# One Strassen level in the second feed-forward of a two-block transformer kernel

## The chip, the cores and the metric

One core of a Trainium2 chip runs the whole kernel in one launch. The metric is the device time of one execution in microseconds (us). Times are medians of several executions; the profile is one execution of its own, so its span differs a little from the median.

## What is computed

Two transformer blocks on 1024 tokens of width 1024, all in float32. The first has two attentions and a gated feed-forward, the second two mixers (a gated spatial one and a gated linear attention) and the feed-forward that is changed here:

```python
    h = h + rmsnorm(m, post_mix_g[l])
    f = rmsnorm(h, pre_ff_g[l]) @ w_ff1[l]
    f = jnp.square(jax.nn.relu(f)) @ w_ff2[l]
    h = h + rmsnorm(f, post_ff_g[l])
```

`w_ff1` is 1024 x 4096 and `w_ff2` is 4096 x 1024. Every product is kept close to float32 by splitting each operand into a rounded part (hi) and the rest (lo), both of type float32r, and adding three products: hi x hi, hi x lo and lo x hi.

## The kernel before

`mm3` (L153 to L156) issues the three matmuls of one 128x128 block of weights against 512 moving columns, so all matmuls of the feed-forward have lines 154, 155 and 156. A split is a copy (hi) and a subtraction (lo): for weights that is `split_rows` (L158 to L167), for transposed tokens `to_T` (L186 to L196), for the hidden values L1413 and L1414.

The second output product (L1350 to L1392) goes over eight token tiles t. For each it does 16 `out2` groups of three matmuls into a 1024-wide PSUM tile (two buffers), then on the vector and scalar engines a root mean square over the tile (L1386, `rstd_ssq`), scaling (L1388), the residual (L1389), a store of the new residual to DRAM (L1390) and the norm of the next stage (`Norm`, L836 and L838). While tile t+1 is multiplied, at group `X_FIN` = 15, `pend.finish()` transposes tile t with eight transposes on the tensor engine and splits it into `hcur`, the token operand of the feed-forward. The token operand thus grows along with the product, and tile 7 is finished after the first hidden blocks have begun (L1416 to L1420).

The second feed-forward (L1403 to L1499) takes the 32 blocks of 128 hidden columns in pairs, the last four together. For a pair, `ff1` (L1406) makes hidden x token tiles: per half of the tokens and per block, 8 `mm3` into one PSUM bank, then relu and square on the scalar engine (L1411, L1412), hi on the vector engine and lo on GpSimd. `ff2` (L1437) multiplies them with two rows of blocks of `w_ff2`: for each token tile t 4 `mm3`, and L1463 adds the PSUM tile to `fr[t]`, which stays in SBUF. Hidden values never leave the chip. The weights of the next pair are loaded (512 KB each, queue SP) and split while the current pair is multiplied. The last four blocks (L1465 on) end each token tile with the last norm (L1490 to L1498) and the store (L1499).

Matmuls of the feed-forward: 32 x 2 x 8 x 3 = 1536 for the first product and 32 x 8 x 2 x 3 = 1536 for the second, 3072 in all.

The program text is an order of issue, but the order in which each engine's stream was laid out is a scheduler's: it places instructions by when it expects their inputs and buffers, and the finished streams are fixed. A pool of tiles that is opened with `reuse_waits="tile"` waits for the former users of its bytes tile by tile; one without waits for all of the former pool.

## Time and profile before

| what | us |
|---|---|
| median of 3 runs | 2654.95 (2654.71 to 2658.44) |
| span of the profiled execution | 2657.4 |
| tensor engine busy in it | 2590.0 |
| start of the last matmul of the second output product | 1926.89 |
| start of the last matmul of the program | 2648.60 |

In the rows below PE is the tensor engine's matmuls, PEld its weight loads, DVE the vector engine, ACT the scalar engine, POOL GpSimd and SP the engine whose queue issues most DMAs. Matmuls overlap, so their pace is read from the distance of their starts and not from their durations.

### The profile page before, as it was taken

To read this page: it belongs to the slowest core of one execution; us is meant where nothing else is said; L and a number is where in the kernel's file an instruction comes from. 1 tells how busy PE (TensorE), PEld (TensorE's weight loads), DVE (VectorE), ACT (ScalarE), POOL (GpSimd) and SP (SyncE) were. 2 spreads that over 40 slices of the span, in tenths; PEclk is the share of its full clock that TensorE was granted. 3 is DMA by queue.
4 is the path that set the end of the run, shared out by engine and by line. 5 is a ranking of instruction groups with operands and counts; after the bars stand their busy time and mean duration, and the time that the engine had idled before them with its cause. 6 is when DMAs were issued, how large, how long until landed. Compare 5 with 4: busy or idle time off the path is not lost.

```text
span 2657.4 us, 34289 instructions
## 1 busy us (share of the span) xinstructions
PE 2590.0 (97%) x13228; PEld 2141.1 (81%) x13228; DVE 1310.0 (49%) x2790; ACT 958.4 (36%) x2241; POOL 589.8 (22%) x447
## 2 busy tenths in 40 slices
PE   7999999988899999999999999999999999999998
PEld 4889999977778888888888788777877878787886
DVE  7977878889763222222222423538544343333325
ACT  4776767778332111111111432345331111111122
POOL 2300000033124333333332210102022121212214
PEclk9999999999999999999999999999999999999999
DMA  7101212231523111111110230212231111111102
GB/s 264 45 28 54 61 52 64 64 99 52 185 75 92 48 48 48 48 48 48 48 48 9 94 87 1 68 40 72 88 127 48 48 48 48 48 48 48 48 32 103
DMA packets 147423, 174.20 MB, mean 66 GB/s; under 512 B 13342, under 2 KB 113582, under 8 KB 146236
## 3 DMA queue, kind: packets, MB, share of 16 engines
q1 hardware_dynamic: 144092, 160.48, 19.3%
q0 software_dynamic: 3168, 11.54, 1.3%
q8 instruction: 104, 1.70, 0.3%
q14 instruction: 59, 0.48, 0.1%
HBM read 155.19 MB, written 16.79 MB: 65 GB/s over the span
## 4 chain that ended last, share of the span: by engine, by line
PE 83%; DVE 8%; ACT 5%; issue 2%; DMA 1%; POOL 1%; SPq 0%; DVEq 0%; ACTq 0%; POOLq 0%
PE acc L154 15%; PE acc L156 14%; PE acc L155 14%; PE wide L154 9%; PE wide L156 9%; PE wide L155 9%; PE acc L601 2%; PE tr L577 2%; PE wide L543 2%; ACT qT L151 1%; PE tr L191 1%; ACT prob L564 1%; PE wide L283 1%; PE acc L615 1%; DVE fr L1498 1%
## 5 line engine op out<-in xcount | busy, mean ns | idle before, releaser
L156 PE MATMUL acc<-hT,slab 128*128 128x512 f32 x1216 | 480.2, 395 | 0.2 <-DVE slab L167 0.2
L154 PE MATMUL acc<-hT,slab 128*128 128x512 f32 x1216 | 479.2, 394 | 0.3 <-ACT hT L195 0.3
L155 PE MATMUL acc<-hT,slab 128*128 128x512 f32 x1216 | 479.4, 394 | 0.0
L154 PE MATMUL wide<-slab 128*128 128x512 f32 x1088 | 431.3, 397 | 1.0 <-DVE fr L1461 0.5
L156 PE MATMUL wide<-slab 128*128 128x512 f32 x1088 | 430.6, 396 | 1.1 <-POOL slab L911 1.1
L155 PE MATMUL wide<-slab 128*128 128x512 f32 x1088 | 428.2, 394 | 0.0
L164 ACT CAST slab<-st 128x1024 fp32r<-128x1024 f32 (+1 forms) x148 | 152.4, 1046 | 562.6 <-PE wide L156 449.6
L167 POOL TENSOR_TENSOR slab<-st,slab 128x1024 fp32r<-128x1024 f32 (+1 forms) x104 | 250.4, 2413 | 438.3 <-ACT slab L164 421.8
L155 PEld LDWEIGHTS acc<-hT,slab 128*128 128x128 f32 x1216 | 228.3, 188 | 54.8 <-DVE hT L196 0.4
L156 PEld LDWEIGHTS acc<-hT,slab 128*128 128x128 f32 x1216 | 228.3, 188 | 54.2 <-DVE slab L167 0.6
L154 PEld LDWEIGHTS acc<-hT,slab 128*128 128x128 f32 x1216 | 228.2, 188 | 54.2 <-ACT hT L195 0.6
L154 PEld LDWEIGHTS wide<-slab 128*128 128x128 f32 x1088 | 204.5, 188 | 54.5 <-DVE fr L1463 5.4
L156 PEld LDWEIGHTS wide<-slab 128*128 128x128 f32 x1088 | 204.7, 188 | 47.8 <-POOL slab L911 1.9
L155 PEld LDWEIGHTS wide<-slab 128*128 128x128 f32 x1088 | 204.6, 188 | 46.2
L1413 DVE CAST slab<-h 128x512 fp32r<-128x512 f32 x60 | 69.9, 1165 | 249.8 <-ACT h L1412 249.8
L1463 DVE TENSOR_TENSOR fr<-wide,fr 128x1024 f32<-128x1024 f32 x104 | 127.1, 1223 | 126.7 <-PE wide L156 125.8
L908 DVE TENSOR_TENSOR h<-h,acc 128x512 f32<-128x512 f32 x44 | 30.2, 687 | 305.0 <-PE acc L156 305.0
L983 DVE TENSOR_TENSOR xr<-wide,xr 128x1024 f32<-128x1024 f32 x88 | 107.7, 1224 | 134.9 <-PE wide L156 134.7
L154 PE MATMUL acc<-wi,slab 128*128 128x384 f32 (+1 forms) x480 | 167.9, 350 | 2.6 <-DVE y L142 1.3
L1414 POOL TENSOR_TENSOR slab<-h,slab 128x512 fp32r<-128x512 f32 x60 | 78.3, 1306 | 406.9 <-DVE slab L1413 406.9
L155 PE MATMUL acc<-wi,slab 128*128 128x384 f32 (+1 forms) x480 | 160.9, 336 | 0.5 <-DVE wi L235 0.5
L156 PE MATMUL acc<-wi,slab 128*128 128x384 f32 (+1 forms) x480 | 160.2, 335 | 0.2 <-POOL slab L327 0.2
(415 smaller groups left out, 4336.6 us busy)
## 6 DMA issues: line engine op xcount, KB each, us to landing
st<-in_w_ff_dram SPq DMA_DIRECT2D x62, 512.0 KB
wm<-in_w_mod_dram SPq DMA_DIRECT2D x48, 256.0 KB
st<-in_w_gate_dram SPq DMA_DIRECT2D x22, 512.0 KB
st<-in_w_up_dram SPq DMA_DIRECT2D x22, 512.0 KB
st<-in_w_down_dram SPq DMA_DIRECT2D x22, 512.0 KB
...
st<-in_w_in_dram SPq DMA_DIRECT2D x12, 512.0 KB
```

Source lines behind the costliest of these rows:

```text
L154: pe.matmul(ps, lhsT=l_hi, rhs=r_hi, start=first, stop=False)
L155: pe.matmul(ps, lhsT=l_hi, rhs=r_lo, start=False, stop=False)
L156: pe.matmul(ps, lhsT=l_lo, rhs=r_hi, start=False, stop=last)
L164: act.copy(w[:, 0], st)
L167: (pool if lo_eng == "pool" else dve).tensor_tensor(w[:, 1], st, fview(w[:, 0]), ALU.subtract)
L543: pe.matmul(Sps[:, o : o + ln], lhsT=qT[:, w_, :], rhs=R.kT[self.kh][:, src : src + ln], start=(w_ == 0), stop=(w_ == 1))
L577: pe.transpose(t[:, (j - b0) * P : (j - b0 + 1) * P], self.P_t[:, j * P : (j + 1) * P], ident)
L601: pe.matmul(OT, lhsT=R.V[self.kh][:, vt, :], rhs=self.PT[j // 4][:, j % 4].rearrange("p e t -> p (e t)"), start=(j == 0), stop=(j == nk_al ...
L983: dve.tensor_tensor(xr[t], ps, xr[t], ALU.add)
L1413: dve.tensor_copy(dst[:, 0, :], h)
L1414: pool.tensor_tensor(dst[:, 1, :], h, fview(dst[:, 0, :]), ALU.subtract)
L1463: dve.tensor_tensor(fr[t], ps, fr[t], ALU.add)
```

## The change

The second feed-forward is computed with one level of Strassen's scheme. For each product the operands are cut into 2 x 2 quarters, and seven quarter products of sums and differences of quarters stand for eight. `A_OF` and `B_OF` name the sums, `UP_SEQ` and `DOWN_SEQ` the order. Splitting into hi and lo now comes after the sums.

First product: the hidden blocks are taken in 16 pairs p. `Tokens` holds the seven sums of token quarters, each [128, 4, 2, 512], for the whole stage. `Cols` loads the columns of a pair (1 MB) and makes their seven sums (`make`). `up_product` is 4 `mm3` into one PSUM bank; `Quarters.take` adds the bank into the four quarters of the result (X, Y) and applies relu and square. `spill` then forms the seven sums that the second product needs of them and stores these to DRAM (`scr2`), 7 x 256 KB for each pair.

Second product: `down_product` goes through the seven quarter products one after another. For each of its 16 pairs, `prepare` loads the stored sum (256 KB) and one or two quarter blocks of `w_ff2` (256 KB each), adds the two, and splits both into a slab; four token tiles then take one `mm3` each, and `take` adds the four PSUM banks into the result rows `acc`. `rows_done` is the last norm and the store.

The token operands are made at two places: `Tokens.first` (tiles 0 to 3) in the output product where `finish` was, and `Tokens.second` (tiles 4 to 7), after the output product, from tiles that are held in SBUF. The PSUM pool is closed and opened anew (`psq`, six banks "m" and two "tr") between the two. `big`, eight tiles of 4 KB a partition, takes the place of several older buffers (`xr`, `blk`), and the buffers of weights (`slab_a`, `slab_b`) are closed before the feed-forward. Lines that only took out debugging or comments are left out here.

```diff
--- before.py
+++ after.py
+UP_LO = {4: "p", 2: "d", 1: "d", 5: "p", 7: "d", 3: "d", 6: "p"}
+UP_TMP = 4
+DOWN_SLABS = 10
...
+    big_pool = ctx.enter_context(tc.tile_pool(name="big", bufs=8, side="right", reuse_waits="tile"))
+    rs = ExitStack()
+    rt = rs.enter_context(tc.tile_pool(name="rt", bufs=2, side="right", reuse_waits="tile"))
+    def big():
+        return big_pool.tile([P, D], F32, tag="big", name="big")
...
-        G[t] = blk.tile([P, 512], F32, tag="blk", name="G")
+        ag = big()
+        A[t], G[t] = ag[:, 0:512], ag[:, 512:1024]
...
+    A_OF = {1: (11, "+", 22), 2: (21, "+", 22), 3: (11,), 4: (22,), 5: (11, "+", 12), 6: (21, "-", 11),
+            7: (22, "-", 12)}
+    B_OF = {1: (11, "+", 22), 2: (11,), 3: (22, "-", 12), 4: (21, "-", 11), 5: (22,), 6: (11, "+", 12),
+            7: (21, "+", 22)}
+    UP_SEQ = (4, 2, 1, 5, 7, 3, 6)
+    DOWN_SEQ = (3, 1, 4, 7, 5, 2, 6)
+    SCR = {1: 0, 3: 1, 4: 2, 5: 3, 2: 4, 6: 5, 7: 6}
+    def alu(sign):
+        return ALU.add if sign == "+" else ALU.subtract
+    def hi_lo(hi, lo, src, lo_eng):
+        act.copy(hi, src)
+        eng(lo_eng).tensor_tensor(lo, src, fview(hi), ALU.subtract)
+    class Tokens:
...
+        def turn(self, y):
+            ts = []
+            for b0 in (0, 4):
+                t = tr_ps()
+                for k in range(4):
+                    pe.transpose(t[:, k * P : (k + 1) * P], y[:, (b0 + k) * P : (b0 + k + 1) * P], ident)
+                ts.append(t)
+            return ts
...
+        def first(self, j, y, tmp):
+            t11, t21 = self.turn(y)
+            raw = self.raw[j] = big()
+            act.copy(raw[:, 0:512], t11)
+            act.copy(raw[:, 512:1024], t21)
+            hi_lo(*self.out(2, j), self.view(t11), "d")
+            d = tmp()
+            dve.tensor_tensor(d, t21, raw[:, 0:512], ALU.subtract)
+            hi_lo(*self.out(4, j), self.view(d), "d")
+        def second(self, j, y, tmp):
+            t12, t22 = self.turn(y)
+            r11, r21 = self.raw[j][:, 0:512], self.raw[j][:, 512:1024]
+            c = tmp()
+            act.copy(c, t12)
+            s1 = tmp()
+            dve.tensor_tensor(s1, t22, r11, ALU.add)
+            hi_lo(*self.out(1, j), self.view(s1), "p")
+            hi_lo(*self.out(5, j), self.view(t22), "d")
+            s7 = tmp()
+            dve.tensor_tensor(s7, t22, r21, ALU.add)
+            hi_lo(*self.out(7, j), self.view(s7), "d")
+            s3 = tmp()
+            dve.tensor_tensor(s3, t22, c, ALU.subtract)
+            hi_lo(*self.out(3, j), self.view(s3), "p")
+            s6 = tmp()
+            dve.tensor_tensor(s6, t12, r11, ALU.add)
+            hi_lo(*self.out(6, j), self.view(s6), "d")
+    class Cols:
+        def __init__(self, src, p, raw_pool):
+            self.raw = raw_pool.tile([P, KT, 2 * P], F32, tag="raw", name="raw", bufs=2)
+            sync.dma_start(self.raw, src[:, p * 2 * P : (p + 1) * 2 * P].rearrange("(k p) f -> p k f", p=P))
+            self.S = {}
...
+        def make(self, i, pool_, bufs, tmp):
+            s = self.S[i] = pool_.tile([P, 2, 4, P], F32R, tag="s", name="s", bufs=bufs)
+            of = A_OF[i]
+            src = self.q(of[0])
+            if len(of) > 1:
+                d = tmp().rearrange("p (k f) -> p k f", k=4)
+                dve.tensor_tensor(d, src, self.q(of[2]), alu(of[1]))
+                src = d
+            hi_lo(s[:, 0], s[:, 1], src, UP_LO[i])
+    def up_product(w, T, i):
+        ps = psp.tile([P, 512], F32, tag="m", name="m", bufs=6)
+        s, t = w.S[i], T.T[i]
+        for k in range(4):
+            mm3(ps, s[:, 0, k, :], s[:, 1, k, :], t[:, k, 0, :], t[:, k, 1, :], k == 0, k == 3)
+        return ps
+    class Quarters:
...
+        def take(self, i, ps):
+            lo, hi = slice(0, 512), slice(512, 1024)
+            if i == 4:
+                self.c = big()
+                act.copy(self.c[:, hi], ps)
+            elif i == 2:
+                self.X = big()
+                dve.tensor_tensor(self.X[:, hi], ps, self.c[:, hi], ALU.add)
+                act.copy(self.c[:, lo], ps)
+                self.done(self.X[:, hi], 0, 1)
+            elif i == 1:
+                self.Y = big()
+                dve.tensor_tensor(self.X[:, lo], ps, self.c[:, hi], ALU.add)
+                dve.tensor_tensor(self.Y[:, hi], ps, self.c[:, lo], ALU.subtract)
+            elif i == 5:
+                self.c = big()
+                dve.tensor_tensor(self.X[:, lo], self.X[:, lo], ps, ALU.subtract)
+                act.copy(self.c[:, lo], ps)
+            elif i == 7:
+                dve.tensor_tensor(self.X[:, lo], self.X[:, lo], ps, ALU.subtract)
+                self.done(self.X[:, lo], 0, 0)
+            elif i == 3:
+                dve.tensor_tensor(self.Y[:, lo], self.c[:, lo], ps, ALU.subtract)
+                dve.tensor_tensor(self.Y[:, hi], self.Y[:, hi], ps, ALU.subtract)
+                self.done(self.Y[:, lo], 1, 0)
+            else:
+                dve.tensor_tensor(self.Y[:, hi], self.Y[:, hi], ps, ALU.add)
+                self.done(self.Y[:, hi], 1, 1)
+    def spill(scr, p, X, Y, c):
+        lo, hi = slice(0, 512), slice(512, 1024)
+        sync.dma_start(scr[SCR[3], p], X[:, lo])
+        sync.dma_start(scr[SCR[4], p], Y[:, hi])
+        s52 = big()
+        dve.tensor_tensor(s52[:, lo], X[:, lo], X[:, hi], ALU.add)
+        dve.tensor_tensor(s52[:, hi], Y[:, lo], Y[:, hi], ALU.add)
+        sync.dma_start(scr[3:5, p].rearrange("i q c -> q i c"), s52.rearrange("q (i c) -> q i c", i=2))
+        dve.tensor_tensor(c[:, hi], X[:, lo], Y[:, hi], ALU.add)
+        sync.dma_start(scr[SCR[1], p], c[:, hi])
+        d67 = big()
+        dve.tensor_tensor(d67, Y, X, ALU.subtract)
+        sync.dma_start(scr[5:7, p].rearrange("i q c -> q i c"), d67.rearrange("q (i c) -> q i c", i=2))
+    def down_product(scr, n_pairs, W, slabs, stage, rows_done):
+        acc = {}
+        def prepare(i, p):
+            cmb = stage.tile([P, 2, 512], F32, tag="cmb", name="cmb", bufs=6)
+            sync.dma_start(cmb[:, 0, :], scr[SCR[i], p])
+            of = B_OF[i]
...
+            if len(of) == 1:
+                block(of[0], cmb[:, 1, :])
+            else:
+                raw = stage.tile([P, 2, 512], F32, tag="wraw", name="wraw", bufs=6)
+                block(of[0], raw[:, 0, :])
+                block(of[2], raw[:, 1, :])
+                dve.tensor_tensor(cmb[:, 1, :], raw[:, 0, :], raw[:, 1, :], alu(of[1]))
+            s = slabs.tile([P, 2, 2, 512], F32R, tag="slab", name="slab", bufs=DOWN_SLABS)
+            hi_lo(s[:, 0], s[:, 1], cmb, "d")
+            return s
+        def mm(ps, s, tt, p):
+            tok = slice(tt * P, (tt + 1) * P)
+            mm3(ps, s[:, 0, 0, tok], s[:, 1, 0, tok], s[:, 0, 1, :], s[:, 1, 1, :], p == 0, p == n_pairs - 1)
...
+        def take(i, tt, ps):
+            u, v = tt, tt + 4
+            if i == 3:
+                acc[u], acc[v] = big(), big()
+                act.copy(half(u, 1), ps)
+            elif i == 1:
+                act.copy(half(u, 0), ps)
+                dve.tensor_tensor(half(v, 1), ps, half(u, 1), ALU.subtract)
+            elif i == 4:
+                dve.tensor_tensor(half(u, 0), ps, half(u, 0), ALU.add)
+                act.copy(half(v, 0), ps)
+            elif i == 7:
+                dve.tensor_tensor(half(u, 0), half(u, 0), ps, ALU.subtract)
+            elif i == 5:
+                dve.tensor_tensor(half(u, 0), half(u, 0), ps, ALU.subtract)
+                rows_done(u, 0, acc[u])
+                dve.tensor_tensor(half(u, 1), ps, half(u, 1), ALU.subtract)
+                rows_done(u, 1, acc[u])
+            elif i == 2:
+                dve.tensor_tensor(half(v, 0), ps, half(v, 0), ALU.add)
+                dve.tensor_tensor(half(v, 1), half(v, 1), ps, ALU.subtract)
+                rows_done(v, 0, acc[v])
+            else:
+                dve.tensor_tensor(half(v, 1), ps, half(v, 1), ALU.add)
+                rows_done(v, 1, acc[v])
+        for n, i in enumerate(DOWN_SEQ):
+            tags = ("m", "m", "m", "m") if n % 2 == 0 else ("m", "m", "tr", "tr")
+            ps = [psp.tile([P, 512], F32, tag=tag, name=tag, bufs=6 if tag == "m" else 2) for tag in tags]
+            cut = n_pairs - (4 if n == 6 else 0)
+            for p in range(cut):
+                s = prepare(i, p)
+                for tt in range(4):
+                    mm(ps[tt], s, tt, p)
+            rest = [(p, prepare(i, p)) for p in range(cut, n_pairs)]
+            for tt in range(4):
+                for p, s in rest:
+                    mm(ps[tt], s, tt, p)
+                take(i, tt, ps[tt])
...
+            for p in range(2):
+                cols[p] = Cols(I["w_ff1_2"], p, wr_pool)
+                for i in (4, 2):
+                    cols[p].make(i, wr_pool, 4, tmp4)
...
-            if pend and i == X_FIN:
-                pend.finish()
+            if pend and i == X_FIN and pend.t < 4:
+                tokens.first(pend.t, pend.y, tmp4)
...
-        y = st4b()
+        y = st3()[:, :D] if t < 4 else big()
...
+    sa.close()
+    ps_s.close()
+    ps_s = ExitStack()
+    psp = ps_s.enter_context(tc.tile_pool(name="psq", bufs=2, space=bass.MemoryType.PSUM))
+    N2 = NF2 // 2
+    scr2 = dram.tile([7, N2, P, 512], F32, name="scr2")
+    with tc.tile_pool(name="up", bufs=1, reuse_waits="tile") as up:
+        def tmp_up():
+            return up.tile([P, 512], F32, tag="tmp", name="tmp", bufs=UP_TMP)
+        tokens.add(up, (1, 5, 7, 3, 6))
+        for j, y in enumerate(held):
+            tokens.second(j, y, tmp_up)
+        for i in UP_SEQ[2:]:
+            cols[0].make(i, up, 5, tmp_up)
+        def squares(h, g, f):
+            act.activation(h, h, AF.Relu)
+            act.activation(h, h, AF.Square)
+        for p in range(N2):
+            if p + 1 < N2 and p + 1 not in cols:
+                cols[p + 1] = Cols(I["w_ff1_2"], p + 1, wr_pool)
+            q = Quarters(squares)
+            for i in UP_SEQ:
+                q.take(i, up_product(cols[p], tokens, i))
+                if p + 1 < N2 and i not in cols[p + 1].S:
+                    cols[p + 1].make(i, *((wr_pool, 4) if i in (2, 4) else (up, 5)), tmp_up)
+            spill(scr2, p, q.X, q.Y, q.c)
+    us.close()
+    with tc.tile_pool(name="stage", bufs=1, side="right", reuse_waits="tile") as stage, \
+            tc.tile_pool(name="down", bufs=2, reuse_waits="tile") as dn:
+        fg = row_bcast(dn, I["post_ff_g_2"], D, "fg", 1)
+        ssqs, xts = {}, {}
...
+            if c == 0:
+                ssqs[t] = dn.tile([P, 8], F32, tag="ssq8", name="ssq8", bufs=8)
+                xts[t] = dn.tile([P, D], F32, tag="xt", name="xt", bufs=4)
+                sync.dma_start(xts[t], x3_scr[t * P : (t + 1) * P, :])
```

## Rows read from the trace of the kernel before

**Rows 1.** The head of the page: the span, and each engine's busy time, share of the span and number of instructions.

```profile
span 2657.4 us, 34289 instructions
...
PE 2590.0 (97%) x13228; PEld 2141.1 (81%) x13228; DVE 1310.0 (49%) x2790; ACT 958.4 (36%) x2241; POOL 589.8 (22%) x447
```

**Rows 2.** Busy time by stretch. Columns: stretch, its length, then busy time (instructions) of PE, PEld, DVE, ACT and POOL, the granted clock of PE, the busy share of the DMA engines, and GB/s. The stretches are seven tiles of the second output product, the begin of the feed-forward, its even part, and its end.

```profile
1850.00:1937.00 87.00, 86.81 (x424) 71.20 (x422) 54.68 (x118) 33.37 (x70) 4.20 (x6) 1.00 0.26 91
1937.00:2002.00 65.00, 64.12 (x277) 50.91 (x276) 26.61 (x24) 20.77 (x28) 22.78 (x13) 1.00 0.38 122
2002.00:2600.00 598.00, 597.61 (x2562) 479.67 (x2561) 218.00 (x185) 113.63 (x160) 131.00 (x83) 1.00 0.15 45
2600.00:2658.00 58.00, 48.21 (x205) 37.35 (x203) 36.44 (x73) 14.45 (x42) 25.82 (x23) 0.97 0.34 118
```

**Rows 3.** Timeline of PE in the even part: start, duration, instruction. The first and the last of 57 matmuls that follow each other.

```profile
2049.69 0.40 PE L155 MATMUL wide<-slab 128*128 128x512 f32 x1
...
2062.76 0.40 PE L154 MATMUL wide<-slab 128*128 128x512 f32 x1
```

**Rows 4.** Groups of instructions by line and shape in the feed-forward (1930 us to the end): out<-in, shapes, count, then busy us and mean ns of one, then idle time of the engine before them and what ended it.

```profile
L1463 DVE TENSOR_TENSOR fr<-wide,fr 128x1024 f32<-128x1024 f32 x104 | 127.1, 1223 | 126.7 <-PE wide L156 125.8
...
L1414 POOL TENSOR_TENSOR slab<-h,slab 128x512 fp32r<-128x512 f32 x60 | 78.3, 1306 | 406.9 <-DVE slab L1413 406.9
...
L164 ACT CAST slab<-st 128x1024 fp32r<-128x1024 f32 x62 | 63.4, 1044 | 272.4 <-PE wide L156 266.6 <-DMA st<-in_w_ff_dram 5.8
L1412 ACT ACTIVATE h<-h 128x512 f32<-128x512 f32 x64 | 40.5, 633 | 1.1
L167 DVE TENSOR_TENSOR slab<-st,slab 128x1024 fp32r<-128x1024 f32 x32 | 38.3, 1234 | 14.0 <-ACT slab L164 14.0
L1411 ACT ACTIVATE h<-acc 128x512 f32<-128x512 f32 x64 | 38.2, 597 | 260.3 <-PE acc L156 260.3
...
L1490 DVE TENSOR_TENSOR fr<-wide,fr 128x512 f32<-128x512 f32 x16 | 11.0, 685 | 4.3 <-PE wide L156 4.1
```

**Rows 5.** Timeline of the seam between the output product and the feed-forward: the transposes of tile 6, the last matmul of the output product, and what tile 7 goes through after it.

```profile
1925.55 1.03 PE L191 MATMUL tr<-ident,st4b 128*128 128x128 f32 x8
...
1926.89 0.39 PE L156 MATMUL wide<-slab 128*128 128x512 f32 x1
...
1927.38 1.03 ACT L1386 ACTIVATE st4b<-wide 128x1024 f32<-128x1024 f32 x1
...
1929.81 1.28 DVE L1388 SCALAR_TENSOR_TENSOR st4b<-wide,r,pmg 128x1024 f32<-128x1024 f32 x1
...
1931.13 1.22 DVE L1389 TENSOR_TENSOR xt<-xt,st4b 128x1024 f32<-128x1024 f32 x1
...
1935.20 1.28 DVE L838 SCALAR_TENSOR_TENSOR st4b<-xt,r,pfg 128x1024 f32<-128x1024 f32 x1
```

**Rows 6.** Timelines that show order: the SP queue around the seam, the scalar engine there (the split of the second weight block, and the norm of tile 7), and the vector engine in the even part.

```profile
1844.38 64.56 SPq L1390 DMA_DIRECT2D x_scr<-xt  x6
1909.05 0.38 SPq L1360 DMA_DIRECT2D st4b<-in_w_ff_dram  x1
1920.45 0.32 SPq L1390 DMA_DIRECT2D x_scr<-xt  x1
...
1929.40 1.05 ACT L164 CAST slab<-st4b 128x1024 fp32r<-128x1024 f32 x1 [0.49 <-DMA st4b<-in_w_ff_dram]
...
1932.44 1.06 ACT L836 ACTIVATE st4b<-xt 128x1024 f32<-128x1024 f32 x1 [1.99 <-DVE xt L1389]
...
2021.17 2.35 DVE L167 TENSOR_TENSOR slab<-st,slab 128x1024 fp32r<-128x1024 f32 x2
2027.05 0.43 DVE L1413 CAST slab<-h 128x512 fp32r<-128x512 f32 x1 [3.53 <-ACT h L1412]
```

**Rows 7.** Line 969 of the first feed-forward, a vector operation with both inputs in SBUF beside GpSimd's splits: count, duration min/median/max in ns.

```profile
L969 DVE TENSOR_TENSOR st<-st,tab x22: 1215/1878/2855, 797.9 to 1419.9; 128x1024 f32<-128x1024 f32 x22
```

**Rows 8.** DMA: two stretches with queued loads of 512 KB in rows of 4 KB, one with the output's stores of 256 KB in rows of 2 KB (columns as in rows 2); the time that one such store holds the SP queue (min/median/max ns); and from the page's list of DMA issues a 512 KB load with its time from issue to landing.

```profile
680.00:684.00 4.00, 4.00 (x19) 3.22 (x19) 2.60 (x3) 1.35 (x3) 0.00 (x0) 1.00 1.02 413
684.00:688.00 4.00, 4.00 (x19) 3.24 (x18) 2.23 (x8) 2.82 (x7) 0.52 (x1) 1.00 1.03 416
2622.00:2640.00 18.00, 18.00 (x78) 14.12 (x77) 14.06 (x29) 5.55 (x18) 10.03 (x10) 1.00 0.54 189
...
L1499 SPq DMA_DIRECT2D out_dram<-fr x16: 332/332/344, 2613.5 to 2654.0; - x16
...
st<-x_scr POOLq DMA_DIRECT2D x8, 512.0 KB, 4.1
```

**Rows 9.** The granted clock of PE around a gap in the prologue (columns as in rows 2).

```profile
81.00:84.00 3.00, 1.05 (x6) 0.84 (x7) 3.00 (x15) 1.92 (x8) 0.72 (x1) 0.96 0.16 61
84.00:87.00 3.00, 3.00 (x11) 2.83 (x12) 3.00 (x12) 2.72 (x9) 1.86 (x3) 0.50 0.00 0
```

**Rows 10.** The end of the program: a matmul ten steps before the last and the last, the last token tile's sum, and its scaling.

```profile
2646.29 0.39 PE L155 MATMUL wide<-slab,hid 128*128 128x512 f32 x1
...
2648.60 0.40 PE L156 MATMUL wide<-slab,hid 128*128 128x512 f32 x1
...
2649.22 0.68 DVE L1490 TENSOR_TENSOR fr<-wide,fr 128x512 f32<-128x512 f32 x1
...
2652.55 1.42 DVE L1498 SCALAR_TENSOR_TENSOR fr<-fr,r,st 128x512 f32<-128x512 f32 x2
```

208 lines of the change are left out of this document (60 added, 148 removed).

## The prediction

> **What bounds the kernel now.** I read the head of the page first: matmuls run in 97% of the span [rows 1], so a second saved is one that the tensor engine (PE) no longer needs, or nothing. Then the stretches [rows 2]: in the feed-forward's even part PE is busy 597.6 of 598.0 us, while the vector engine (DVE) has 36% and the scalar engine (ACT) 19% of it and the DMA engines 15%. Nothing else is near a limit there. The length of the feed-forward is therefore its count of matmuls times their pace. The pace is in the timeline [rows 3]: 56 steps in 13.07 us, 0.2334 us each. 3072 x 0.2334 = 717.0; from the last matmul of the output product (1926.89 + 0.23 = 1927.1 [rows 5]) to the end of the program's last (2648.83 [rows 10]) are 721.7. So the whole feed-forward holds only 4.7 us that are not its matmuls, 1.0 of them the transposes of tile 7. From the last matmul to the end of the span are another 8.6 us. This accounting is the one the change has to be put through.
>
> **What is removed.** Seven quarter products for eight: each product becomes 16 x 7 x 12 = 1344 matmuls of the same shape, 2688 in all, 384 fewer. 384 x 0.2334 = 89.6 us, all of it on the path. The pace is my first assumption: weight blocks and moving columns keep their shape, so I keep it. The last ten steps before the end ran at 0.231 (2646.29 to 2648.60 [rows 10]); over 2688 matmuls that would be 6.5 us less.
>
> **What moves.** The transposes of tiles 4, 5 and 6 leave the output product: three times 1.03 us [rows 5], so that product ends at about 1924.0. They come back behind it: `second` transposes four tiles, 4.1 us of PE.
>
> **The first seam** is where I expect most of the loss. Before, PE went on with the first hidden block at once, since the token operand had grown beside the product. Now product 1 needs its sum over all four tiles 4 to 7, and nothing but transposes and products 4 and 2 can run before. (a) The PSUM pool is opened anew, so PE waits until tile 7's last PSUM reader, L1388, is through: 1927.1 to 1931.1 in the rows, 4.0 us [rows 5]. (b) Then each `second` costs DVE five operations with one input in PSUM (0.685 for 512 columns [rows 4]) and two wholly in SBUF (half of 1.234 [rows 4], 0.617): 4.66 us, four times 18.6. Beside it DVE owes tile 7 its 1.22 and 1.28 [rows 5] and some 0.8 of small steps (my estimate: ACT's 1.06 and these fill the 2.8 us between L836 and L838 [rows 5, 6]); the two transposed banks are reused from tile to tile, which adds a bubble of some 0.5 us each. The sum for product 1 of the last tile is third in its list and then goes through ACT (0.52) and GpSimd (1.31 [rows 4]). It is there about 24 to 26 us after the output product's end; I take 25. (c) In these 25 us PE has 4.1 of transposes and, with products 4 and 2 of the first pair, 5.6 of matmuls; if the scheduler also brings the second pair's 4 and 2 forward, 11.2. Idle: 15 or 10 us. I take 14; bounds 9 and 25 (all of it idle). [...]
>
> **The first product** has room. For one pair PE needs 84 x 0.2334 = 19.6 us. DVE: 5 sums and 4 splits in SBUF and, in `spill`, three sums of 512 columns and one of 1024, 14 x 0.617 = 8.6; 8 operations from PSUM, 8 x 0.685 = 5.5; 14.1 us. ACT: 7 rounded copies (0.52), 3 from PSUM (0.60), four relus and squares (0.63 each): 10.5. GpSimd: 3 x 1.31 = 3.9. DMA: 1 MB in, 1.8 MB out, 2.9 MB in 19.6 us = 146 GB/s. SP's stores of the sums wait for the pair's last square; behind them in its queue stands the next pair's load, which has a buffer of its own and a whole pair of time. With six PSUM banks PE can be five products ahead. I cost it at nothing; the cover is the 5.5 us that DVE has left.
> What could take that cover: a DVE operation with both inputs in SBUF took 1.88 us (median; 1.22 at least, 2.86 at most) beside GpSimd [rows 7], against 1.22 from PSUM [rows 4]. [...]
>
> **The second seam** is soft: loads and weight sums of the second product depend on nothing late, and the streams are not in program order (a weight load was issued at 1909 ahead of the tile-6 store at 1920, ACT split a later weight at 1929 ahead of tile 7's norm at 1932, DVE split weights at 2021 ahead of that group's own hidden copies at 2027 [rows 6]). If they were, the store of the last sums, a load and a split would be in line, 5 + 4.1 + 2.9 = 12 us. I take 3, bounds 0 and 12.
>
> **The second product.** A step (12 matmuls) is 2.80 us of PE. DVE 0.62 + 1.23 = 1.85, ACT 1.04. DMA: in five of seven products 768 KB, 786 kB / 2.80 us = 281 GB/s, in two 512 KB. No row shows this load. Queued 512 KB pieces in 4 KB rows ran at 413 to 416 GB/s with the engines' share at 1.0; 256 KB stores in 2 KB rows made 189 GB/s of a share of 0.54, 350 when scaled up [rows 8]. Both lie above 281; the pieces here are the second kind, so I take 350 and a cover of a fifth. SP's issue is 3 x 0.33 = 1.0 us a step [rows 8]; the eight residual loads that move to it from GpSimd's queue add 0.33 each. Six steps of loads and ten slabs stand ahead of PE. At the end of each quarter product DVE owes four `take`s (2.7 us; about 14 in product 5, 5.5 and the last norm's 4 x 2.2), which ten slabs (28 us) hide if they are ahead. I take 3 us for the six transitions, bounds 0 and 45.
>
> **The end.** Before, the last tile's sum began at 2649.2 and its scaling ended at 2654.0 [rows 10]. Now four tiles end 2.80 us apart, while DVE has 0.69 + 1.42 + 0.8 = 2.9 of work for each and the chain through ACT takes 4.8; 0 to 3.4 us longer, I take 1.4, so 10.0 from last matmul to end.
>
> **The sum**: 1924.0 + 14 + 2 + 4.1 + 2688 x 0.2334 (627.4) + 3 + 3 = 2577.5; + 10.0 = 2587.5 of span. That is 69.9 under 2657.4. The runs' median 2654.95 lies 2.4 under the profiled span; I take the difference over: 2654.95 - 69.9 = **2585**.
>
> **Rivals.**
> (B) The fixed streams put the conversions of the next quarter product behind the `take`s of the last. Then PE stands at each of six transitions for 4 x 0.69 + 0.62 + 1.04 + 1.23 = 5.6 us, and 11 more after product 5: 45, in place of 3, gives 2627. For it: DVE's stream is one queue and a `take` that waits for PE blocks what is behind it. Against: rows 6, and the 4.7 us of all waits in the present feed-forward.
> (C) DVE becomes the bound of the first product. If each of its 13 SBUF operations met GpSimd and lost the 0.66 us of rows 7's median, 14.1 + 8.6 = 22.7 us a pair, 3.1 over PE, and 16 pairs 50 us: 2635. Against: GpSimd works a fifth of the time.
> (D) The other side: the second product goes at the pace of its loads. The point from which it is slower than before is a step of 2.80 + 70/112 = 3.43 us, or 207 GB/s on the whole 79.7 MB. It decides whether transfers overlap. If the loads of one step waited to land before the next ones were issued, 4.1 us as in rows 8, the step is 1.3 too long, and 112 of them 146 us: 2731. For it: three transfers a step in 2 KB rows, a queue that also has to wait for buffers, and never so much traffic for so long in this trace. Against: rows 8, and six steps of buffers. [...]
> (E) The loads' pace lies just so that it eats the gain: a step within 0.05 of 3.43. No change.
>
> **Chances.** Forecast 0.67, B 0.13, C 0.07, D 0.08, E 0.02, and 0.03 for a load pace that costs some 20 to 60 us and leaves a gain. The measurement tells about 0.2% (5 us) from no change. Faster: 0.67 + 0.13 + 0.07 + 0.03 = 0.90; same 0.02; slower 0.08. The forecast's own range from its bounds: with the first seam at 9, nothing for clock, seam two and transitions, 8.6 at the end and a pace of 0.231 it is 2564; with 25, 4, 12 and 3.4 it is 2609. With B the range is 2564 to 2628, which holds 0.80; C and D lie outside.
>
> **What would show it.** Right: PE starts 0.2334 us apart in both products; a gap of some 14 us at about 1930 to 1955 with products 4 and 2 in it; no idle PE in the pairs with DVE near 72%; in the second product DMA at 254 GB/s in the mean (79.7 MB in 314 us) and a share under 0.9. B shows as six gaps of 5 us or more, 45 us apart, that end at a split. C shows as PE waiting for DVE in every pair, with two-input operations near 1.9 us. D shows as a DMA share near 1.0, or PE waiting for `cmb` and `wraw` loads in every step. The forecast is wrong if PE's pace changes, if the first seam is longer than 25 us, or if stages ahead of 1850 us move because older buffers now share bytes.

## The result, and the profile after

The changed kernel takes 2587.74 us (median of 4 runs, 2586.4 to 2590.93) against 2656.06 for the kernel before in the same comparison (4 runs, 2654.71 to 2658.44): ratio 0.9741, 95% interval 0.9728 to 0.9755. The forecast was 2585.0 with a range from 2564 to 2628. The profiled execution has a span of 2584.6 us; 2587.5 was the forecast for it.

The head of the page after (columns as in [rows 1]):

```profile
span 2584.6 us, 34817 instructions
...
PE 2491.0 (96%) x12844; PEld 2076.6 (80%) x12844; DVE 1506.5 (58%) x3148; ACT 1119.9 (43%) x2485; POOL 509.9 (20%) x401
```

PE runs 384 matmuls fewer and is busy 99.0 us less, more than the 89.6 forecast for them. Stretches of the changed kernel (columns as in [rows 2]): the end of the output product, the first seam, the piece behind it with a granted clock of 0.54, the first product, the second seam, the second product, the end.

```profile
1850.00:1925.60 75.60, 75.56 (x364) 61.74 (x362) 48.14 (x104) 29.87 (x65) 4.37 (x6) 1.00 0.24 84
1925.60:1961.30 35.70, 13.00 (x57) 10.54 (x57) 27.19 (x44) 19.14 (x35) 11.47 (x8) 0.69 0.04 15
1961.30:1967.00 5.70, 5.70 (x14) 4.09 (x15) 5.70 (x7) 2.41 (x5) 3.18 (x2) 0.54 0.00 0
1967.00:2250.00 283.00, 283.00 (x1247) 233.71 (x1246) 215.93 (x312) 154.28 (x265) 57.75 (x44) 1.00 0.44 147
2250.00:2276.00 26.00, 23.12 (x99) 18.03 (x98) 16.76 (x22) 10.63 (x15) 0.00 (x0) 1.00 0.90 309
2276.00:2560.00 284.00, 284.00 (x1254) 235.25 (x1253) 203.88 (x239) 123.22 (x147) 18.07 (x12) 1.00 0.83 287
2560.00:2584.60 24.60, 12.64 (x56) 10.14 (x54) 13.84 (x32) 3.71 (x12) 5.53 (x4) 0.86 0.23 85
```

Both products keep PE busy without a gap, at 283.00 / 1247 = 0.2269 and 284.00 / 1254 = 0.2265 us a matmul; the even part before had 597.61 / 2562 = 0.2333 [rows 2]. The first seam is 36 us long and PE works 13 of them. All waits of PE from 1900 to 2590 us, with the sum, the number and the longest:

```profile
PE tr L1372 <- DVE tmp L1404: 10.8, 3, 5.4
PE m L159 <- ACT s L1349: 8.0, 1, 8.0
PE tr L1372 <- DVE big L1598: 4.0, 1, 4.0
PE m L159 <- ACT slab L1349: 1.6, 1, 1.6
PE m L160 <- DVE slab L1350: 1.2, 1, 1.2
```

The first three are the first seam (22.8 us), the last two the second (2.8). There is none at the six transitions. PE's timeline gives the ends of the stages: the output product's last matmul, the transposes of the four held tiles, one after another, and the program's last matmul.

```profile
1925.16 0.40 PE L161 MATMUL wide<-slab 128*128 128x512 f32 x1
1929.52 1.94 PE L1372 MATMUL tr<-ident,big 128*128 128x128 f32 x8 [3.96 <-DVE big L1598]
...
1944.77 1.94 PE L1372 MATMUL tr<-ident,big 128*128 128x128 f32 x8 [5.40 <-DVE tmp L1404]
1951.31 1.94 PE L1372 MATMUL tr<-ident,big 128*128 128x128 f32 x8 [4.59 <-DVE tmp L1404]
...
2572.26 0.39 PE L161 MATMUL m<-slab 128*128 128x512 f32 x1
```

A tile takes 6.5 us there. What DVE does for one (timeline of DVE, the second held tile and the begin of the third):

```profile
1940.86 0.68 DVE L1397 TENSOR_TENSOR tmp<-tr,big 128x512 f32<-128x512 f32 x1
1942.74 0.69 DVE L1350 TENSOR_TENSOR T<-tr,T 128x512 fp32r<-128x512 f32 x1 [1.20 <-ACT T L1349]
1943.35 0.68 DVE L1401 TENSOR_TENSOR tmp<-tr,big 128x512 f32<-128x512 f32 x1
...
1944.54 0.68 DVE L1407 TENSOR_TENSOR tmp<-tr,big 128x512 f32<-128x512 f32 x1
1945.14 2.36 DVE L1350 TENSOR_TENSOR T<-tmp,T 128x512 fp32r<-128x512 f32 x2
1947.42 0.68 DVE L1397 TENSOR_TENSOR tmp<-tr,big 128x512 f32<-128x512 f32 x1
```

Seven operations 0.60 us apart are 4.2 us. Another 1.2 are spent waiting for ACT: its rounded copy for product 5 (1942.13) stands in its stream behind the one for product 1 (1941.62), which waits for DVE's first sum. The last two operations, wholly in SBUF, take 2.36 us together instead of 1.28, beside a GpSimd row of 1.60 us that begins at 1945.36.

Span by terms, from the rows above (forecast in brackets): output product to 1925.4 (1924.0, +1.4, which says little: eleven profiles of kernels that are the same up to there start its last matmul between 1919.1 and 1926.8); 1344 x 0.2269 + 1344 x 0.2265 = 609.4 of matmuls (627.4, -18.0); second seam and transitions 1.98 + 1.61 us between starts, less two steps, 3.1 (6, -2.9); from the last matmul's end at 2572.5 to the end of the span 12.1 (10.0, +2.1); what is left of 2584.6 is put down to the first seam, 34.6 (14 + 2 + 4.1 = 20.1, +14.5). The sum is -2.9, from 2587.5 to 2584.6. Two terms were far off and cancelled. The experiments are about these two, and about the rivals that did not come.

### The profile page after: what moved, and what is told of

It reads as the page before. It is cut to its first block, busy times and chain, and to the rows that moved or that the text cites. A ratio compares the mean times of both kernels' runs of the same rounds, so it can differ in the third digit from the quotient of the medians.

```text
span 2584.6 us, 34817 instructions
## 1 busy us (share of the span) xinstructions
PE 2491.0 (96%) x12844; PEld 2076.6 (80%) x12844; DVE 1506.5 (58%) x3148; ACT 1119.9 (43%) x2485; POOL 509.9 (20%) x401
## 4 chain that ended last, share of the span: by engine, by line
PE 68%; DVE 3%; ACT 1%; DMA 1%; issue 1%; POOL 0%; SPq 0%; DVEq 0%; ACTq 0%
PE acc L161 8%; PE acc L159 8%; PE acc L160 8%; PE m L160 7%; PE m L161 7%; PE m L159 7%; PE wide L159 6%; PE wide L161 6%; PE wide L160 6%; PE tr L196 1%; PE tr L160 1%; PE tr L161 1%; PE tr L159 1%; DMA wraw<-in_w_ff_dram 0%; PE wide L1186 0%
## 5 line engine op out<-in xcount | busy, mean ns | idle before, releaser
L161 PE MATMUL acc<-hT,slab 128*128 128x512 f32 x704 | 277.6, 394 | 0.0
L160 PE MATMUL acc<-hT,slab 128*128 128x512 f32 x704 | 277.4, 394 | 0.0
L159 PE MATMUL acc<-hT,slab 128*128 128x512 f32 x704 | 277.3, 394 | 0.0
L172 POOL TENSOR_TENSOR slab<-st,slab 128x1024 fp32r<-128x1024 f32 (+1 forms) x74 | 177.4, 2406 | 350.8 <-ACT slab L169 334.5
L161 PE MATMUL wide<-slab 128*128 128x512 f32 x608 | 240.7, 396 | 1.1 <-POOL slab L916 1.1
L159 PE MATMUL wide<-slab 128*128 128x512 f32 x608 | 241.1, 397 | 0.3 <-ACT slab L200 0.2
L160 PE MATMUL wide<-slab 128*128 128x512 f32 x608 | 240.5, 396 | 0.0
L169 ACT CAST slab<-st 128x1024 fp32r<-128x1024 f32 (+1 forms) x86 | 89.1, 1048 | 293.4 <-PE wide L161 183.2
L984 DVE TENSOR_TENSOR big<-wide,big 128x1024 f32<-128x1024 f32 x88 | 107.8, 1225 | 135.0 <-PE wide L161 134.8
L159 PE MATMUL m<-T,s 128*128 128x512 f32 x448 | 176.1, 393 | 8.0 <-ACT s L1349 8.0
L1349 ACT CAST slab<-cmb 128x1024 fp32r<-128x1024 f32 x112 | 114.1, 1047 | 146.4 <-DVE cmb L1509 63.9
L161 PE MATMUL m<-T,s 128*128 128x512 f32 x448 | 175.7, 392 | 0.0
L160 PE MATMUL m<-T,s 128*128 128x512 f32 x448 | 175.6, 392 | 0.0
L1350 DVE TENSOR_TENSOR slab<-cmb,slab 128x1024 fp32r<-128x1024 f32 x112 | 136.8, 1249 | 64.4 <-ACT slab L1349 61.2
L160 PEld LDWEIGHTS acc<-hT,slab 128*128 128x128 f32 x704 | 132.2, 188 | 30.8
L159 PEld LDWEIGHTS acc<-hT,slab 128*128 128x128 f32 x704 | 132.2, 188 | 30.7
L161 PEld LDWEIGHTS acc<-hT,slab 128*128 128x128 f32 x704 | 132.3, 188 | 30.5
L593 DVE TENSOR_TENSOR PT<-tr,PT 128x512 fp32r<-128x512 f32 x231 | 129.4, 564 | 43.9 <-ACT PT L592 41.8
```

Of the source, the lines that this page charges most:

```text
L159: pe.matmul(ps, lhsT=l_hi, rhs=r_hi, start=first, stop=False)
L160: pe.matmul(ps, lhsT=l_hi, rhs=r_lo, start=False, stop=False)
L161: pe.matmul(ps, lhsT=l_lo, rhs=r_hi, start=False, stop=last)
L169: act.copy(w[:, 0], st)
L172: (pool if lo_eng == "pool" else dve).tensor_tensor(w[:, 1], st, fview(w[:, 0]), ALU.subtract)
L593: dve.tensor_tensor(PT[:, :, 1, :], src, fview(PT[:, :, 0, :]), ALU.subtract)
```

## The experiments

Each median is over the runs of that kernel; ratios are to the kernel before, run beside it (2656 to 2657.5 us). The runs of one kernel spread by 1 to 8 us, so medians 3 us apart are not told apart. Where less is at stake the stage is read in the trace. For the first seam that is the length from the start of the output product's last matmul to the start of the first product's last one: 338.7 us in the changed kernel, and 338.6 to 338.8 in the six other profiles with the same seam.

### Half of the change undone: eight quarter products in the second product

`down_product` runs 4 x 32 steps with one load of a stored quarter and one weight block each; `spill` stores the four quarters and builds no sums. The two mixed quarters change places when they are read back, so this kernel computes something else; no instruction or byte hangs on that. In part:

```
-  for n, i in enumerate(DOWN_SEQ):            # 7 x 16 steps
+  for n, (h, c) in enumerate(((0, 0), (0, 1), (1, 0), (1, 1))):   # 4 x 32 steps
-  sync.dma_start(cmb[:, 0, :], scr[SCR[i], p])
+  sync.dma_start(cmb[:, 0, :], scr[2 * k + h, p])
```

> The second product alone goes back to eight quarter products: the four quarters of the middle values are stored as they are, each of 4 x 32 steps loads 512 KB, 1536 matmuls for 1344, takes are plain copies. If PE sets the pace of both products (my theory), the 192 matmuls come back at the 0.227 us that the changed kernel shows: +43.6 us, 2631 us (2627 to 2635), and the pace in the second product stays near 0.227. Rival, the seven-product form loses time to its heavier loads and seven transitions that I don't see in the waits: then eight products cost less than 43.6, below 2622. Second rival, the faster pace of the changed kernel comes from the seven-product form itself: then these matmuls fall back to 0.2334 and it is 1536 x 0.0065 = 10 us more, 2641.

Measured: 2625.49 us, ratio 0.9886 (0.9871 to 0.9901): 37.8 more than the changed kernel, between theory and rival. All waits of PE from 2250 us on:

```profile
PE m L159 <- ACT slab L1349: 0.4, 1, 0.4
PE m L160 <- DVE slab L1350: 0.3, 1, 0.3
```

The matmuls do come back at 0.2265 us (43.5). Of the second seam's 3.1 us 2.5 are gone, the end is 1.2 shorter (10.9), and this execution left the output product 1.1 earlier: 43.5 - 4.8 = 38.7, the difference in span. So the second half of the change earns its matmuls less some 4 us of seam and end. Its pace is that of the seven-product form, which refutes the second rival.

### The first seam: banks, order, or DVE's work

Early copies: both transposed banks are copied to the dead `y` tile by ACT, and the sums read the copies. In part:

```
   t12, t22 = self.turn(y)
-  c = tmp()
-  act.copy(c, t12)
+  act.copy(y[:, 0:512], t12)
+  act.copy(y[:, 512:1024], t22)
+  t12, t22 = y[:, 0:512], y[:, 512:1024]
```

> At the first seam the transposes of each held tile are copied at once from PSUM to SBUF (two ACT copies for one), and all sums read the copies, so that the two PSUM banks come free early; nothing else changes. If the banks' turn-round is what took 6.5 us per tile there (my theory), the four tiles go at the pace of DVE's own work, product 1 starts near 1952 instead of 1961.3, and the kernel takes 2577 to 2581 us. Rival, DVE's work bounds the seam (27.2 us busy of 35.7): product 1 not before 1958, 2584 to 2588 us.

Measured: 2584.82 us, ratio 0.9741 (0.9723 to 0.9759). PE's waits at the seam became one of 20.3 us beside the 4.0 of tile 7, 24.3 for 22.8, and the seam's length is 339.1 for 338.7 us: no gain, as the rival had it. DVE no longer waits for ACT from the second tile on, and yet a tile takes 6.4 us. What took the place of that wait is in the rows of DVE there (line, operation, tiles, count: min/median/max ns, first and last start):

```profile
L1350 DVE TENSOR_TENSOR T<-tmp,T x8: 675/678/680, 1934.6 to 1955.9; 128x512 fp32r<-128x512 f32 x8
L1398 DVE TENSOR_TENSOR tmp<-big x4: 684/1744/1779, 1929.4 to 1947.9; 128x512 f32<-128x512 f32 x4
L1402 DVE TENSOR_TENSOR tmp<-big x4: 687/1746/1749, 1930.0 to 1950.8; 128x512 f32<-128x512 f32 x4
```

The same sums took 676 to 684 ns (L1397) and 681 ns (L1401) in the changed kernel, where one input was in PSUM. L1397 met no GpSimd row there and L1401 only the last 0.2 us of one. But the low part for product 5, which reads PSUM too, took its 0.69 us at 1942.74 (above) wholly inside one:

```profile
1942.30 1.27 POOL L1350 TENSOR_TENSOR T<-tmp,T 128x512 fp32r<-128x512 f32 x1 [1.91 <-ACT T L1349]
```

```profile
L1401 DVE TENSOR_TENSOR tmp<-tr,big x4: 681/681/681, 1936.8 to 1956.4; 128x512 f32<-128x512 f32 x4
```

And the timeline of the run with the copies shows beside what they are long:

```profile
1934.77 1.62 POOL L1350 TENSOR_TENSOR T<-tmp,T 128x512 fp32r<-128x512 f32 x1 [1.28 <-ACT T L1349]
1935.17 1.78 DVE L1398 TENSOR_TENSOR tmp<-big 128x512 f32<-128x512 f32 x1
...
1937.68 1.60 POOL L1350 TENSOR_TENSOR T<-tmp,T 128x512 fp32r<-128x512 f32 x1 [1.29 <-ACT T L1349]
1938.08 1.75 DVE L1402 TENSOR_TENSOR tmp<-big 128x512 f32<-128x512 f32 x1
```

Each long row begins inside a GpSimd row and ends some 0.55 us behind it, nearly its own length. The copies took the sums out of PSUM, and so put them under this hold-up: from the second tile on two rows of each lose 1.07 us where one did.

Early copies, and no GpSimd: the low parts for products 1 and 3 go to DVE (`"p"` becomes `"d"` in two calls of `hi_lo`).

> As the run with the early copies, but the eight low parts of the held tiles' sums that GpSimd made there (for products 1 and 3) are made by DVE, so GpSimd has almost nothing to do at the seam. The trace of that run showed DVE's sums of two SBUF tiles at 1.74 to 1.80 us wherever a GpSimd row ran and at 0.68 elsewhere. My theory (a GpSimd row holds up a DVE row whose operands are all in SBUF until it ends, 1.07 us each time): twelve long rows give back some 11 us, the eight low parts add 8 x 0.60 = 4.8, the kernel takes 4 to 7 us less than that run, 2578 to 2581 us. Rival, the long rows are long for another reason and GpSimd did real work for DVE: 4.8 us more, 2589 us.

Measured: 2581.28 us, ratio 0.9715 (0.9700 to 0.9729), 3.5 less than with the copies alone, just short of my 4 to 7; the seam's length is 335.3 us, 3.8 less. The direction is the theory's; the rival asked for 4.8 more. A group of DVE's rows and PE's wait there:

```profile
L1398 DVE TENSOR_TENSOR tmp<-big x4: 687/692/695, 1932.9 to 1948.6; 128x512 f32<-128x512 f32 x4
```

```profile
PE m L159 <- ACT s L1349: 17.3, 1, 17.3
```

A GpSimd row of 1.6 us saved DVE 0.60 us and cost it 1.07. The sums that began inside a GpSimd row took 1.75 us and ended behind it; without the row they take 0.69 us. The rows with one input in PSUM, 0.69 us wholly inside a GpSimd row, show the way round it.

Built quarter by quarter: the sums of product 1 for all four tiles first, then 7, 6, 5 and 3; products 4 and 2 of two pairs and product 1 of the first are emitted ahead. In part:

```
-  for j, y in enumerate(held): tokens.second(j, y, tmp_up)
+  for j, y in enumerate(held): tokens.second(j, y)        # transposes and copies
+  early = {(p, i): up_product(cols[p], tokens, i) for p in range(2) for i in (4, 2)}
+  build(1)
+  early[0, 1] = up_product(cols[0], tokens, 1)
+  build(7); build(6); build(5)                             # 3 before its product
```

> As the run with the early copies, and the sums are built quarter by quarter (the tokens of product 1 for all four tiles, then of 7, 6, 5 and 3) with products 4 and 2 of pairs 0 and 1 and product 1 of pair 0 ahead of them, so that PE has five products (13.6 us) to do while DVE builds. My theory (the seam is an order of work, not an amount of it): 12 to 18 us less than the changed kernel, 2570 to 2576 us. Rival, DVE's 27 us of sums plus the takes bound the seam whatever the order: PE stops as long, only later, and the gain is under 5 us, over 2582.

Measured: 2587.04 us, ratio 0.9738 (0.9724 to 0.9753). PE waited 4.0 + 11.7 + 5.0 = 20.7 us, 2 less than in the changed kernel, and the seam's length is 338.4 us: the rival, under 5. The same with the eight low parts that GpSimd made (products 1 and 5) on DVE:

> As the run with the sums built quarter by quarter, but the eight low parts that GpSimd made there (for products 1 and 5) are made by DVE. My theory (hold-up by GpSimd): the DVE rows of that seam were 9 us longer in sum than at 0.68 us each, the eight low parts cost 4.8 us, so 4 to 6 us less than that run, 2581 to 2583 us, and the 12 us stop ahead of product 5 shrinks to 7 or less. Rival (GpSimd did real work for DVE): 4.8 us more, 2592 us.

Measured: 2579.37 us, ratio 0.9709 (0.9694 to 0.9723): 7.7 less than with GpSimd and 8.4 less than the changed kernel. The seam's length is 332.8 us, 5.6 less than with GpSimd, inside my 4 to 6; the rest of the 7.7 lies within the spread of the runs. The long stop shrank from 11.7 to 5.5 us (7 or less forecast). All waits of PE at the seam:

```profile
PE m L159 <- ACT s L1349: 5.5, 1, 5.5
PE m L159 <- ACT T L1349: 5.0, 1, 5.0
PE tr L1372 <- DVE big L1594: 4.0, 1, 4.0
...
PE m L160 <- DVE T L1350: 0.9, 1, 0.9
```

15.4 us for 22.8. By the seam's length the new order gains 0.7 us over the copies alone while GpSimd works there, and 2.5 us when it does not (332.8 for 335.3). The order pays only when DVE is not held up: neither of my first two theories was whole.

### The second product: loads and cover

256 KB more in each step, into a tile that nobody reads:

```
   sync.dma_start(cmb[:, 0, :], scr[SCR[i], p])
+  more = stage.tile([P, 512], F32, tag="more", name="more", bufs=4)
+  sync.dma_start(more, scr[SCR[i], p])
```

> In the second product every step loads 256 KB more (the sum of the middle values a second time, into a tile that nobody reads), so five of seven products load 1 MB a step and two 768 KB. My theory (loads are hidden, but with little margin: the windows' highest mean is 364 GB/s at a DMA share of 1.02): at 364 GB/s a step of 1049 KB takes 2.88 us for the 2.73 us of its twelve matmuls, at 330 it takes 3.18, so 80 steps cost 12 to 36 us, less the lead of ten slabs: 2598 to 2622 us, with PE waiting for slabs. Rival, the limit is at the 405 GB/s and more that other windows showed, a step fits into 2.73 us, and the time stays within 2 us of 2587.

Measured: 2628.83 us, ratio 0.9901 (0.9886 to 0.9916), 41 more: my direction, beyond my range. Stretches of products with 1 MB a step (columns as in [rows 2]; the takes of product 5 lie in the last):

```profile
2276.00:2320.00 44.00, 41.71 (x167) 30.12 (x168) 26.86 (x30) 16.70 (x19) 0.00 (x0) 1.00 1.03 379
...
2370.00:2420.00 50.00, 48.20 (x198) 35.53 (x198) 31.61 (x36) 18.50 (x21) 0.00 (x0) 1.00 0.99 351
...
2470.00:2515.00 45.00, 35.30 (x150) 28.84 (x149) 25.18 (x36) 18.01 (x32) 9.88 (x8) 0.91 0.66 244
```

The first two show the DMA engines busy throughout, at a share of 1.03 and 0.99, while they move 379 and 351 GB/s in these 256 KB pieces. PE's waits from 2250 us on are 20 us more than in the changed kernel. One of them is rival B's stop. DVE's timeline and PE's:

```profile
2499.35 0.69 DVE L1537 TENSOR_TENSOR big<-big,m 128x512 f32<-128x512 f32 x1 [13.02 <-PE m L161]
...
2510.69 1.21 DVE L1350 TENSOR_TENSOR slab<-cmb,slab 128x1024 fp32r<-128x1024 f32 x1
```

```profile
2511.95 0.79 PE L160 MATMUL m<-slab 128*128 128x512 f32 x1 [9.70 <-DVE slab L1350]
```

DVE stands at a take of product 5 until PE has finished it, and the split that PE needs next is behind the takes and the row work. The fixed stream has this order; what hides it is the lead that the loads build up. The other half of the 41 us is not in stops of this kind: 131 matmuls start 0.25 to 0.70 us after the one before them, where the changed kernel has five such steps. They cost 20 us, part of it at the lower granted clock (0.85 in the mean from 2512 to 2530 us), and the end is 3.2 us longer. What makes each of them long is open.

Three slabs for ten (`DOWN_SLABS = 3`):

> In the second product three slabs for ten, so the conversions can be at most three steps (8.2 us) ahead of PE. My theory (the ten slabs' lead is what hides the takes and the next product's first loads at the six transitions): PE stops at several of them, 1 to 3 us each and more behind product 5, whose eight takes and row work stand in DVE's stream: 2592 to 2607 us. Rival, the scheduler's order keeps conversions ahead of the takes and the lead is not needed: within 2 us of 2587.

Measured: 2596.35 us, ratio 0.9776 (0.9761 to 0.9791), 8.6 more, inside my range. PE's waits from 2250 us on:

```profile
PE m L160 <- DVE slab L1350: 5.9, 5, 3.3
PE m L159 <- ACT slab L1349: 1.9, 1, 1.9
```

The two longest of the first line, 3.3 and 1.3 us, are behind product 5; at the other transitions the lead of three steps is nearly enough. Cover was needed where I said, and without seven of the ten slabs it costs 9 us, not the 45 of rival B.

### The pace

64 bytes between the operands, in the second product only:

```
-  s = slabs.tile([P, 2, 2, 512], F32R, tag="slab", ...)
+  s = slabs.tile([P, 2, 1040], F32R, tag="slab", ...)     # hi in 0:512, lo in 512:1024 of each operand
```

> In the second product's slabs the right operand starts 64 bytes further on (1040 elements behind the left one for 1024, and hi and lo of one operand side by side), so that weights and moving rows no longer stand at the same offset within 128 bytes, as they do not in the kernel before; the first product is unchanged and serves for comparison. If the pace of 0.2267 for 0.2334 us comes from the addresses, the second product falls back towards 0.2334: 1344 x 0.0067 = +9 us, 2597 us. Rival (the pace is a pattern set by the last stop of PE, or has to do with something else): the pace stays at 0.2267 and the time within 2 us of 2587.

The same with 128 and with 256 bytes (1056 and 1088 for 1040), one run each:

> As the run with the right operand 64 bytes further on in the slabs of the second product, but 128 bytes further on (1056 elements behind the left one). If the offset within 128 bytes is what counts, the two operands stand alike again and the second product is back at 226.7 ns a matmul, as in the changed kernel. Rival, any departure from the changed kernel's layout (offsets of whole 512 bytes) disturbs the pattern: 229 ns or more, as at 64 bytes.

> The same with the right operand 256 bytes further on (1088 elements behind the left one). If the offset within 128 bytes is what counts: 226.7 ns. If only whole 512 bytes do: 229 ns or more here and at 128 bytes. If whole 256 bytes are enough: 226.7 here and more at 128.

Measured: 2586.99 (ratio 0.9739, 0.9722 to 0.9755), 2590.82 and 2585.66 us. With 64 bytes that is the rival's time and not my 2597. But such steps are within the spread of the runs, and this profile left the output product 3.6 us earlier than the changed kernel's. From the first product's last matmul to the program's last are 308.5 us in the changed kernel, and 313.1, 316.6 and 308.9 with 64, 128 and 256 bytes. From 2300 to 2500 us (columns as in [rows 2]), the changed kernel, then 64, 128 and 256 bytes:

```profile
2300.00:2500.00 200.00, 200.00 (x884) 165.64 (x883) 142.41 (x169) 94.04 (x113) 11.98 (x8) 1.00 0.86 295
```

```profile
2300.00:2500.00 200.00, 200.00 (x873) 163.80 (x872) 139.84 (x165) 92.57 (x111) 12.02 (x8) 1.00 0.84 288
```

```profile
2300.00:2500.00 200.00, 200.00 (x863) 162.13 (x862) 136.55 (x156) 90.12 (x109) 12.03 (x8) 1.00 0.84 287
```

```profile
2300.00:2500.00 200.00, 200.00 (x884) 165.66 (x883) 141.99 (x167) 93.01 (x113) 11.10 (x8) 1.00 0.85 292
```

200 us over 884, 873, 863 and 884 matmuls are 226, 229, 232 and again 226 ns. The distance of moving operand and weights within 256 bytes moves the pace: my 128 was the wrong period, 256 the right one among those tried, and 64 bytes go less than half of the way back to 0.2334 us.

The kernel before, moved by 64 bytes: one unused tile ahead of the pools that grow from the right end of SBUF.

```
+  pad_pool = ctx.enter_context(tc.tile_pool(name="pad", bufs=1, side="right"))
+  pad_pool.tile([P, 16], F32, name="pad")
```

> The kernel before with one unused tile of 64 bytes ahead of the pools that grow from the right end of SBUF, and no other edit: the transposed tokens and the hidden values then stand at the same offset within 128 bytes as the weights they are multiplied with, where they stood 64 bytes off. If the pace comes from the addresses, the 3072 matmuls of the second feed-forward go from 0.2334 towards the 0.2267 us of the changed kernel, and the other matmuls with such operands gain as well: 9 us less at the step that the shifted slabs cost (2.8 ns a matmul), 20 us at the whole difference, 2636 to 2648 us. Rival, the pace belongs to the loops (accumulation in eight against four, or a pattern set by the last stop): 0.233 stays, within 3 us of 2657.

Measured: 2649.08 us, ratio 0.9968 (0.9957 to 0.9980), 8.4 less, just short of my 9 to 20; in the profiles the second feed-forward alone is 4.1 us shorter (717.6 for 721.7). In the same stretch, before and with the tile:

```profile
2300.00:2500.00 200.00, 199.87 (x856) 159.98 (x856) 76.21 (x62) 39.70 (x56) 48.48 (x29) 1.00 0.16 48
```

```profile
2300.00:2500.00 200.00, 199.55 (x863) 161.56 (x862) 79.35 (x64) 36.42 (x51) 44.82 (x27) 1.00 0.15 48
```

233.5 ns became 231.2. In the compiled programs the operands of the feed-forward's matmuls before stood 64 or 192 bytes apart (modulo 256; 864 and 2208 of them), with the tile half of them stand at 0 and half at 128, and in the changed kernel all 2688 stand at 0. By the paces measured for 0 and 128 the mean should be 229.

Most of the other 2 ns are not pace. In the kernel before PE stops for a moment in the second product of each of the twelve pairs between 2002 and 2500 us:

```profile
2044.10 2.38 POOL L167 TENSOR_TENSOR slab<-st,slab 128x1024 fp32r<-128x1024 f32 x1 [1.56 <-ACT slab L164]
2044.58 2.19 DVE L1413 CAST slab<-h 128x512 fp32r<-128x512 f32 x1 [3.42 <-ACT h L1412]
...
2047.95 0.19 PEld L154 LDWEIGHTS wide<-slab 128*128 128x128 f32 x1 [0.40 <-DVE fr L1463]
```

The rounded copy L1413, 0.43 us elsewhere [rows 6], lasts 2.19 beside a GpSimd split, and the sum L1463 behind it, for which PE waits, comes late. PE loses some 0.3 us each time: 3.5 us in all, or 1.4 ns a matmul from 2002 to 2600 us. With the tile it is 1.8 us, or 2.1 ns a matmul, in the stretch above.

With steps over 245 ns left out, the starts of the feed-forward's matmuls can be read one by one, each with the distance of its own operands. Mean step in ns:

| distance | before | before, with the tile | changed kernel's second product, as it is and moved |
|---|---|---|---|
| 0 | | 228.8 | 226.7 (moved by 256: 226.7) |
| 64 | 230.7 | | 229.5 |
| 128 | | 232.2 | 232.4 |
| 192 | 232.7 | | |

The 57 matmuls of [rows 3], from which the forecast took its pace, all stand at 192. With the tile the first product's matmuls at 0 go at 227.2, the pace of the changed kernel, in the loops of the kernel before: so the loops are not the cause there. The second product's at 0 go at 229.5; these 2.8 ns I can't place.

Quarter by quarter, no GpSimd, and the unused tile:

> The run with the sums built quarter by quarter without GpSimd, and the same unused tile of 64 bytes ahead of the right-hand pools: in both products of the second feed-forward the operands stand alike already, so only the gate's and the attention's projections before it change. If addresses set the pace there (about 3000 matmuls at 2.8 ns or more), 2579.4 less 8 to 15: 2564 to 2572 us. Rival: within 3 us of 2579.

Measured: 2576.54 us, ratio 0.9697 (0.9682 to 0.9711), the lowest median here: 11.2 us less than the changed kernel, 2.8 less than without the tile, which the runs can't tell from nothing. That is inside the rival's 3 us, not my 8 to 15. I had priced each matmul of those stages at a full 2.8 ns, and their slabs, 8320 bytes apart, still alternate within 256 bytes: 64 and 192 (229.8 and 233.1 ns) became 0 and 128 (227.8 and 232.5), 1.3 ns in the mean, some 3 us over 2650 matmuls.

## Why the prediction was right, and where it was right by luck

By the signs that the prediction named itself, two of three for "wrong" came: PE's pace changed, and the first seam was longer than 25 us. The third did not: matmul 9000 of the trace starts at 1697.7 us before and at 1696.2 after, within what profiles of kernels that are the same up to there differ by (1693.5 to 1698.3). The range held all the same, and the terms show why.

**What is removed**: right in kind. PE bounds both products, and 192 matmuls put back cost their pace. The pace itself was mis-sized: "weight blocks and moving columns keep their shape, so I keep it". Shape was the same; the tiles' addresses were not. 18.0 us of the gain are the pace. Some 14 of them are the steps themselves: 232.1 ns in the mean before and 227.0 after, without the steps over 245 ns, times 2688. That is mostly the distance of the operands, a gift of tiles that lie at multiples of 256 bytes from each other, and no part of Strassen's scheme; 64 bytes gave the kernel before 8.4 of its own. Some 4 are the short stops of the second product before, 1.4 ns a matmul, which the changed kernel does not have.

**The first seam** was mis-sized: 25 us forecast to product 1, 36.1 measured (1925.16 to 1961.26), 14.5 us on the sum. I had 4.66 us a tile and a "bubble of some 0.5"; the tile took 6.5, of which 1.2 was DVE waiting for ACT and 1.1 GpSimd's hold-up; and the weight sum for product 1 stood behind all four tiles in DVE's stream, so that PE waited 8.0 us after the last transposes. The last token sum for product 1 was whole at 1956.6, the weight sum only at 1961.2. I had the hold-up in [rows 7] before me and applied it to the first product only, where it does not matter, and not to the seam, where DVE has no slack. The step that failed is the pricing of DVE at the seam: its 4.66 us a tile left out the wait for ACT and the hold-up, and the weight sums of the first pair were not counted there at all. Without GpSimd and in the better order the seam takes 5.9 us less. The second pair's products 4 and 2 were not brought forward. Clock: the 2 us in the sum were my estimate, and no run shows that term as I priced it; in its place the profile after shows a granted 0.54 from 1961.3 to 1967, some 2.5 us lost, after PE had worked 13.0 of 35.7 us.

**The first product**: right. PE never stops; DVE is at 216 of 283 us (76%, forecast 72%). Rival C did not come: its hold-ups exist (the weight sums L1428 from two SBUF inputs took 0.69 us in the median there and up to 1.77), but GpSimd works 58 of 283 us and DVE has the room.

**The second seam and the transitions**: 3 us forecast for the seam, 3.1 measured; 3 for the transitions, none measured. Rival B's mechanism is real (the takes do stand in front of the splits; with the heavier loads DVE stood 13.0 us at one) and is hidden by ten slabs and six steps of loads; with three slabs it costs 9 us.

**The second product**: right. The mean is 287 GB/s, at a share of 0.83; the forecast's 254 had left out the residual rows, the output and the other transfers (86.6 MB for 79.7 moved from 2260 to 2575 us). The 351 to 379 GB/s that the heavier loads reached with the share at 1.0 bear out the 350 that I took from [rows 8] and the cover of a fifth; a third more bytes a step already costs 41 us. D's point was far off.

**The end**: 12.1 us for 10.0, at its upper bound of 12.0.

So the forecast lay 2.7 us from the median by luck: +14.5 and -18.0 met. The range would have held the time with either error alone: about 2599.5 or 2567.
